# Two-layer hybrid decoder trunk: new costs in the order planner, and norm sums with one product

## The chip, the cores and the metric

The kernel runs on one core of a Trainium2 chip. The time is that of one launch on the device, in microseconds. Three runs of the kernel before took 1268.65, 1270.82 and 1272.52 us; the median, 1270.82 us, is the time to compare with.

In the profile PE is TensorE's matrix products and PEld its weight loads, DVE is VectorE, ACT ScalarE, POOL GpSimd and SP SyncE, which here issues most transfers (DMA).

## The reference

One sequence of 512 tokens, width 1024, with 16 learned tokens put ahead of it (528 columns), goes through two layers in float32. With `rms(x, g) = x / sqrt(mean(x^2) + 1e-6) * g` a layer is

```python
u = rms(h, pre_g);  z = u @ w_in                 # 1024 x 2824
y_attn = softmax(q k^T / 8 + F[t] - F[s], causal) v   # 8 heads of 64; F = cumsum(log_sigmoid(f + b))
y_conv = silu(layer_norm(conv31(a_val * sigmoid(a_gate)))) @ a_pw_w
y_sc   = sc_b * conv3(sc_c * sc_x)
y = head_norm(concat(y_attn, y_conv, y_sc)) @ w_out
h = h + rms(y, post_g)
z = conv3(rms(h, pre_g) @ w_up);  g, up = split(z)   # 2 x 2816 channels
h = h + rms((silu(g) * up) @ w_down, post_g)
```

All convolutions are causal and by channel. At the end the 16 learned tokens are dropped.

## The kernel before

**Layout.** Activations lie transposed: 128 partitions are 128 channels, the columns are the 528 tokens, worked on as two halves of 264 (`hf` 0 and 1). A float32 product of sufficient precision is made of three fast ones: each operand is split into a high part (a copy that rounds, on ScalarE) and a low part (a subtraction, on VectorE), and high x high, high x low and low x high are added up in PSUM (`mm3`, line 668). Weights come from memory block by block through a transfer on SyncE's queue, a copy on ScalarE (line 608) and a subtraction on VectorE (line 612). For 16 of the 22 channel blocks of the FFN's up projection, seven products of sums and differences stand in for eight (`ups`, line 2198).

**Stages.** An opening (norm of the input), then for either layer: the mixer (`mixer`: projections, attention, convolutions), the output projection with its two norms (`finish`), the FFN, and the FFN's last part with its norms (`finish` again).

**The norms.** `Norms.square` squares a pair of channel blocks (line 749) and adds it to an accumulator `acc` of 2 x 264 columns (line 765); after the last pair `acc` holds two partial sums side by side. `Norms.factor` sums over the channels with a matrix of 1/1024: one product for each of the two halves of `acc`, into the same PSUM columns (line 792). These two products have plain float32 operands. Some sums are taken in parts: with `apart`, the last pairs are not added to `acc` but get products of their own. Behind the sum stand three operations on ScalarE (lines 801 to 805) and two on VectorE (806, 812) that make the reciprocal root. The keys are `("h", hf)` for the norm ahead of a sub-layer and `("y", hf)` for the one behind it.

**The planner.** The order of the instructions on each engine isn't left to a compiler: `Flow` (lines 247 to 368) runs a small model of the chip while the kernel is built. Work for ScalarE, VectorE, GpSimd and SyncE is handed over with `flow.op(engine, us, fn, after, prio, lat)`: `us` is the time that it is thought to hold its engine, `lat` how much later than that its result is there, `after` what it waits for. `Flow.run` takes again and again what can start first, by priority where several can, and emits it; so its order becomes the engine's order. Products on TensorE come from Python generators that yield what they wait for; the first in the list of threads that can go on is emitted. Where the planner sees TensorE without work for longer than a limit, it emits filler products (line 1775), 80% of the gap at 0.225 us each. The chip then runs each engine's list in that order, and an instruction waits until its data are there.

The costs are simple formulas: `act_us(n)` is 0.17 + 0.0009 n, `dve_us(n)` 0.17 + 0.00101 n for n columns; a small transfer (`dma`, line 534) 0.35 us of SyncE. In the mixer a row maximum (`reduce` in `maxima`, line 1368) is booked with `dve_us(n) + 0.08`; the low parts of queries and keys (`low` in `q_proj` and `k_proj`, lines 1292 and 1320) with `dve_us(264)`; and the copy of a query's high part to other partitions with a landing of 2.2 us.

An engine is free for the next operation, in the model, where the one before ends:

```python
self.free[eng] = start + us
tok.time = start + us + lat
```

Of the kernel before, what the change touches and what calls it, by code (L numbers as in the profile page):

```python
# [9 lines left out]
F32 = mybir.dt.float32  # L10
# [10 lines left out]
H = L // 2  # L21
# [34 lines left out]
WE = 0.5  # L56
YS = (9, 9)
NWARM = 10
K1 = 2
SQD = (2, 6)  # L60
FILLED = 0.8
# [7 lines left out]
FILL_US = 0.225  # L69
OH = {(0, 0): -3, (0, 4): -2.9, (0, 6): -2.8, **{(1, k): -0.4 for k in range(0, KD, 2)}}  # L70
OW = (-0.46, -0.459)
ADD_US, ADD_LAT = 1.2, 3.6
PT = ((0.8035, 0.8055), (0.8035, 0.8055))
D0 = ((0, 0, 0, 0, 5, 10, 15, 20), (0, 0, 0, 0, 5, 10, 15, 20))

# [171 lines left out]
class Flow:  # L247
# [1 line left out]

    HOP = 0.06

    def __init__(self):
        self.pe = 0.0
# [52 lines left out]
    def run(self, stop=None):  # L308
        while True:
            if stop is not None and stop():  # L310
                return
            best = None
            for eng, ops in self.pend.items():
                can = [(r + self.HOP, o) for o in ops if (r := self.ready(o[4], o[7])) is not None]
                if can:
                    start = max(self.free[eng], min(r for r, _ in can))
                    o = min((o[0], r, o[1], o) for r, o in can if r <= start)[3]
                    if o[0] >= self.yields:
                        soon = [(r, q[0], q[1], q) for r, q in can if q[0] < o[0] - 0.5 and r < start + 0.6 * o[2]]
                        if soon:  # L320
                            start, _, _, o = min(soon)
                    if best is None or start < best[0]:
                        best = (start, eng, o)
            can = [(r, i) for i, t in enumerate(self.threads) if (r := self.ready(t[1])) is not None]
            if can:
                start = max(self.pe, min(r for r, _ in can))
                if best is None or start < best[0]:
                    best = (start, None, self.threads[min(i for r, i in can if r <= start)])
            if best is None:
                assert not self.threads and not any(self.pend.values()), "nothing can go on"  # L330
                return
            start, eng, o = best
            self.now = start
            if eng is not None:
                self.pend[eng].remove(o)
                _, _, us, fn, _, tok, lat, _, takes = o
                for r, slot in takes:
                    r.take(slot)
                fn()
                self.free[eng] = start + us  # L340
                tok.time = start + us + lat
                continue
            if self.rings and start > self.pe:
                bank = next((r.slots[0].buf for r in self.rings() if r.slots and r.slots[0].buf is not None
                             and (t := r.slots[0].time) is not None and t <= self.pe), None)
                if bank is not None:
                    gap = start - self.pe
                    for _ in range(int(FILLED * (gap - 0.05) / FILL_US) if gap > self.least else 0):
                        self.filler(bank)
            self.pe = max(self.pe, start)  # L350
            try:
                y = next(o[0])
            except StopIteration:
                self.threads.remove(o)
                continue
            o[1] = [Tok(0.0)] if y is None else [Tok(self.pe + y)] if isinstance(y, float) else y
# [30 lines left out]
def tile_hybrid_trunk(ctx: ExitStack, tc: tile.TileContext, xT, wflat, pv_d, out):  # L387
# [144 lines left out]
        return flow.op("pool", us, fn, after, **kw)  # L532

    def dma(out, in_, *after, **kw):
        return flow.op("sp", 0.35, lambda: nc.sync.dma_start(out, in_), after, **kw)

    class Early:

# [180 lines left out]
    class Norms:  # L719


        def __init__(self, pool, rs, nc=4, **apart):
            self.pool, self.nc = pool, nc
            self.c, self.acc = Ring(nc), Ring(2)
            self.factors(rs, **apart)

# [13 lines left out]
        def square(self, key, k, src, n, *after, prio=1, on_dve=False):  # L740

            apart = self.n_apart(key)
            s = self.sums.setdefault(key, {"parts": {}})
            us = act_us(2 * n)
            box, slot = {}, Slot()

            def squares(tile):
                box["c"] = tile()
                nc.scalar.activation(box["c"], src, AF.Square)

            if k == 0:
                a = act(us, lambda: squares(lambda: T(self.pool, [P, 2, H], F32, "acc", 2)[:, :, :n]), *after,
                        prio=prio, takes=[(self.acc, slot)])
                s["acc"], s["at"] = box, a
            else:
                if on_dve:
                    def product():
                        box["c"] = self.c_tile(n)
                        nc.vector.tensor_mul(box["c"], src, src)

                    a = dve(dve_us(2 * n), product, *after, prio=prio, takes=[(self.c, slot)])
                else:
                    a = act(us, lambda: squares(lambda: self.c_tile(n)), *after, prio=prio, takes=[(self.c, slot)])
                if k < KD - 2 * apart:
                    s["at"] = dve(dve_us(2 * n), lambda: nc.vector.tensor_add(s["acc"]["c"], s["acc"]["c"], box["c"]),
                                  a, s["at"], prio=prio)
                    slot.close(s["at"])
            if k == 0 or k >= KD - 2 * apart:
                s["parts"][max(0, k // 2 - KD // 2 + apart + 1) if k else 0] = box, slot
                box["at"] = [a]  # L770
            if k == KD - 2 * apart - 2:
                s["acc"]["at"], s["acc"]["there"] = [s["at"]], True
            return a

        def factor(self, key, n, out=None):
# [8 lines left out]
            for j in range(n_parts):  # L784
                yield [When(lambda: there(j)), When(lambda: self.after.get(key, []))]
                if j == 0:
                    p_slot = yield from flow.grab(pring[0]["n"])
                    ps = psum[:, p_slot.buf, :n]
                s = self.sums[key]
                box, slot = s["parts"][j]  # L790
                for i in range(2):
                    nc.tensor.matmul(ps, lhsT=om_d, rhs=box["c"][:, i, :], start=j + i == 0, stop=j + 1 == n_parts and i == 1)  # L792
                tok = flow.mm(2 * 0.0017 * n)
                slot.close(tok)
            s["free"] = mine = Slot()
            us, vs = act_us(n), dve_us(n)
# [97 lines left out]
    def mixer(l, ypool, first, close_first, spans):  # L894
# [384 lines left out]
        def q_proj(j):  # L1279
# [15 lines left out]
            def use(hf, ps, tok):  # L1295
                out = []
                for hd in (2 * j, 2 * j + 1):
                    c = half_sl(hf)
                    a = act(act_us(H), lambda hd=hd: high(hd, c, ps), tok, prio=0)
                    d = dve(dve_us(H), lambda hd=hd: low(hd, c, ps), a, prio=0)  # L1300
                    q_at.setdefault(hd, [zeros[hd]] if hd in zeros else []).append(a)
                    q2_at.setdefault(hd, []).append(d)
                    out += [a, d]
                return out

            yield from proj(use)
            for hd in (2 * j, 2 * j + 1):
                main = rows(hd)[0]
                q1, q2 = qh[hd % 4]
                q2_at[hd].append(dma(q2[main].bitcast(F32), q1[main].bitcast(F32), *q_at[hd], lat=2.2))  # L1310

        def k_proj(j):
            def high(hd, c, ps):
# [8 lines left out]
            def use(hf, ps, tok):  # L1322
                out = []
                for hd in (2 * j, 2 * j + 1):
                    c = half_sl(hf)
                    a = act(act_us(H), lambda hd=hd: high(hd, c, ps), tok, prio=0)
                    d = dve(dve_us(H), lambda hd=hd: low(hd, c, ps), a, prio=0)
                    q2_at[hd] += [a, d]
                    if hf == 0:
                        k_at[hd, 0] = a  # L1330
                    else:
                        k_at[hd] = [k_at[hd, 0], a]
                    out += [a, d]
# [11 lines left out]
        def maxima():  # L1345

            dm_at = {}
            for hd in range(HEADS):
# [6 lines left out]
                for b, (qs, n) in enumerate(QB):  # L1355
                    end = qs + n
                    pieces = [(0, end)] if end <= 512 else [(0, H), (H, end)]
                    for i, (a, z) in enumerate(pieces):
# [11 lines left out]
                                scalar=-3e38 if i == 0 else mcol[:n, 5:6], op0=ALU.add, op1=ALU.max,  # L1370
                                accum_out=mcol[:n, b:b + 1] if last else mcol[:n, 5:6])

                        d = dve(dve_us(z - a) + 0.08, reduce, tok, prio=0)
                        slot.close(d)
                        yield
                    diag.append(gp(0.5, lambda qs=qs, end=end, n=n, b=b: nc.gpsimd.tensor_scalar(
# [408 lines left out]
    with tc.tile_pool(name="pre", bufs=2, reuse_waits="tile") as sp, tc.manual_schedule(engines=every):  # L1785
# [7 lines left out]
        plan_w(after_mixer[0])  # L1793
        norms = Norms(sp, [T(sp, [P, L], F32, f"rs{i}", 1) for i in range(NRS)], NCS, h=APS)
        norms.apart["h", 0] = KD // 2 - 1
        hg, hg_at = T(sp, [P, KD, L], F32, "hg", 1), {}
        for hf in range(2):
            for k in range(0, KD, 2):
# [10 lines left out]
    for l in range(DEPTH):  # L1809
# [21 lines left out]
        with tc.tile_pool(name=f"fp{l}", bufs=2, reuse_waits="tile") as fp:  # L1831
# [29 lines left out]
            first = First(u_in, iws, {})  # L1861
            rs = T(fp, [P, L], F32, "rs", 1)
            norms = Norms(fp, [rs])
            plan = ExitStack()
            plan.enter_context(tc.manual_schedule(engines=every))
            flow.yields = YF[l]
# [551 lines left out]
            with plan:  # L2418
# [54 lines left out]
                wpos[0] += 2  # L2473
                rs, rz = (T(fp, [P, L], F32, n, 1) for n in ("rs", "rz"))
                norms.factors([rs, rz], h=APART)
                norms.apart["y", 1] = YA[l]
                norms.acc = Ring(2)
                flow.yields = YE[l]
# [60 lines left out]
```

## Time and profile before

| | |
|---|---|
| median of three runs | 1270.82 us (1268.65 to 1272.52) |
| profiled execution | 1272.24 us; span on the core 1270.5 us |
| busy PE | 1237.3 us, 97% of the span |
| busy PEld | 1187.7 us, 93% |
| busy DVE | 969.2 us, 76% |
| busy ACT | 775.3 us, 61% |
| busy POOL | 236.4 us, 19% |
| moved by DMA | 165.85 MB, 131 GB/s |
| mean granted clock of TensorE | 0.995 |

Busy time is the union of an engine's instructions in the profile. Matrix products overlap, and their ends are modelled, so a PE that is busy is not a PE at its peak. Lines such as L792 are lines of the kernel. In a group, `x64` counts instructions, behind the bar stand busy time, mean duration of one in ns, and the idle time of the engine just before them with what ended it. In a timeline a row starts with the time from the span's start and its length.

### The profile page before, as it was taken

To read this page: it belongs to the slowest core of one execution; us is meant where nothing else is said; L and a number is where in the kernel's file an instruction comes from. 1 tells how busy PE (TensorE), PEld (TensorE's weight loads), DVE (VectorE), ACT (ScalarE), POOL (GpSimd) and SP (SyncE) were. 2 spreads that over 40 slices of the span, in tenths; PEclk is the share of its full clock that TensorE was granted. 3 is DMA by queue.
4 is the path that set the end of the run, shared out by engine and by line. 5 is a ranking of instruction groups with operands and counts; after the bars stand their busy time and mean duration, and the time that the engine had idled before them with its cause. 6 is when DMAs were issued, how large, how long until landed. Compare 5 with 4: busy or idle time off the path is not lost.

```text
span 1270.5 us, 24515 instructions
## 1 busy us (share of the span) xinstructions
PE 1237.3 (97%) x9468; PEld 1187.7 (93%) x9468; DVE 969.2 (76%) x1752; ACT 775.3 (61%) x1571; POOL 236.4 (19%) x415
## 2 busy tenths in 40 slices
PE   8999999999999999999999999999998999999996
PEld 8999988999999999999999999889997999999996
DVE  7788877588866777778677888765897578778855
ACT  7257668667755555556673667685586565556552
POOL 1313321002122222120003233200022122112100
PEclk9999999999999999999999999999999999999998
DMA  6132231637486766776341322126376677668641
GB/s 226 51 102 60 63 89 34 218 113 169 106 194 139 191 160 147 170 162 184 114 141 35 95 80 68 56 74 206 128 171 144 155 163 170 165 146 180 142 142 67
DMA packets 73941, 165.85 MB, mean 131 GB/s; under 512 B 8080, under 2 KB 26640, under 8 KB 73312
## 3 DMA queue, kind: packets, MB, share of 16 engines
q1 hardware_dynamic: 52048, 124.86, 30.6%
q0 software_dynamic: 21360, 39.02, 18.9%
q8 instruction: 74, 1.21, 0.4%
q10 hardware_dynamic: 416, 0.40, 0.1%
q14 instruction: 43, 0.35, 0.1%
HBM read 129.14 MB, written 8.65 MB: 108 GB/s over the span
## 4 chain that ended last, share of the span: by engine, by line
PE 80%; DVE 6%; ACT 5%; DMA 5%; issue 3%; POOL 1%; SPq 0%; DVEq 0%; POOLq 0%; ACTq 0%
PE psum L668 37%; PE psum L2198 25%; PE psum L709 6%; PE psum L1204 4%; DMA raw<-in_w_dram 3%; PE psum L1462 2%; PE psum L1405 1%; PE psum L792 1%; DMA c<-acc 1%; PE psum L1361 1%; DVE wlo L612 1%; PE psum L1199 1%; DMA raw<-u 1%; POOL pf L1423 1%; ACT whi L608 1%
## 5 line engine op out<-in xcount | busy, mean ns | idle before, releaser
L668 PE MATMUL psum<-yhi,whi 128*128 128x264 f32 (+3 forms) x660 | 188.3, 300 | 3.1 <-ACT yp L2373 1.7
L668 PE MATMUL psum<-ylo,whi 128*128 128x264 f32 (+3 forms) x660 | 185.2, 295 | 1.1 <-DVE ylo L2175 0.8
L668 PE MATMUL psum<-yhi,wlo 128*128 128x264 f32 (+3 forms) x660 | 184.7, 295 | 0.1
L668 PE MATMUL psum<-uhi,whi 128*128 128x264 f32 (+1 forms) x640 | 165.1, 291 | 1.2 <-DVE q L1292 1.2
L668 PE MATMUL psum<-ulo,whi 128*128 128x264 f32 (+1 forms) x640 | 161.0, 284 | 0.1
L668 PE MATMUL psum<-uhi,wlo 128*128 128x264 f32 (+1 forms) x640 | 160.6, 283 | 0.0
L2124 DVE SCALAR_TENSOR_TENSOR c<-z,pv,c 128x528 f32<-128x528 f32 (+1 forms) x156 | 117.2, 758 | 29.3 <-ACT c L2122 26.5
L612 DVE TENSOR_TENSOR wlo<-raw,whi 128x1024 fp32r<-128x1024 f32 (+2 forms) x84 | 100.5, 1206 | 37.8 <-ACT whi L608 37.7
L668 PEld LDWEIGHTS psum<-yhi,whi 128*128 128x128 f32 x660 | 121.0, 189 | 8.4 <-ACT yp L2373 2.2
L668 PEld LDWEIGHTS psum<-ylo,whi 128*128 128x128 f32 x660 | 121.0, 189 | 4.4 <-DVE ylo L1088 1.1
L668 PEld LDWEIGHTS psum<-yhi,wlo 128*128 128x128 f32 x660 | 121.1, 189 | 3.2 <-DVE wlo L612 0.6
L668 PEld LDWEIGHTS psum<-uhi,whi 128*128 128x128 f32 x640 | 111.9, 188 | 4.3 <-issue 2.4
L668 PEld LDWEIGHTS psum<-ulo,whi 128*128 128x128 f32 x640 | 112.2, 188 | 0.5 <-DVE ulo L1947 0.3
L2211 ACT COPY z<-psum 128x264 f32<-128x264 f32 (+2 forms) x128 | 48.2, 377 | 105.4 <-PE psum L2198 104.7
L668 PEld LDWEIGHTS psum<-uhi,wlo 128*128 128x128 f32 x640 | 112.1, 188 | 0.0
L608 ACT CAST whi<-raw 128x1024 fp32r<-128x1024 f32 (+2 forms) x84 | 85.9, 1035 | 38.9 <-DMA raw<-in_w_dram 21.1
L937 DVE SCALAR_TENSOR_TENSOR cacc<-apad,pv,cacc 128x528 f32<-128x528 f32 x120 | 88.7, 768 | 0.3
L709 PE MATMUL psum<-uhi,whi 128*128 128x264 f32 (+1 forms) x320 | 85.0, 289 | 1.8 <-ACT uhi L840 1.8
L709 PE MATMUL psum<-uhi,wlo 128*128 128x264 f32 (+1 forms) x320 | 83.4, 283 | 0.0
L2052 DVE TENSOR_TENSOR wlo<-raw,whi 128x1024 fp32r<-128x1024 f32 (+4 forms) x78 | 76.6, 982 | 8.9 <-ACT whi L2049 8.3
L2049 ACT CAST whi<-raw 128x1024 fp32r<-128x1024 f32 (+4 forms) x78 | 66.4, 856 | 16.5 <-PE psum L668 10.3
L2198 PE MATMUL psum<-uhi,whi 128*128 128x264 f32 (+1 forms) x256 | 72.7, 284 | 2.2 <-ACT yp L2373 2.2
(317 smaller groups left out, 3729.2 us busy)
## 6 DMA issues: line engine op xcount, KB each, us to landing
raw<-in_w_dram SPq DMA_DIRECT2D x110, 512.0 KB
u<-in_w_dram SPq DMA_DIRECT2D x32, 512.0 KB
u<-in_w_dram POOLq DMA_DIRECT2D x32, 256.0 KB, 5.2
raw<-in_w_dram POOLq DMA_DIRECT2D x32, 256.0 KB, 4.0
u<-raw POOLq DMA_DIRECT2D x32, 256.0 KB, 3.8
raw<-u POOLq DMA_DIRECT2D x32, 256.0 KB, 4.4
raw<-in_w_dram SPq DMA_DIRECT2D x16, 448.0 KB
h_mid<-h SPq DMA_DIRECT2D x4, 1056.0 KB
```

Of the source, the lines that this page charges most:

```text
L608: nc.scalar.copy(box["hi"][:, :sz], box["raw"][:, :sz])
L612: nc.vector.tensor_sub(lo[:, :sz], box["raw"][:, :sz], box["hi"][:, :sz].bitcast(F32))
L668: nc.tensor.matmul(d, lhsT=w[a][:, k, cols], rhs=rhs(b, k, hf), start=start and i == 0 and p == 0, stop=stop and i == n - 1 and p == 2)
L709: nc.tensor.matmul(self.ps[hf, i], lhsT=self.ws[i].w[a][:, k, :], rhs=self.rhs(b, k, hf), start=k + a + b == 0, stop=k == KD - 1 and b == 1)
L937: nc.vector.scalar_tensor_tensor(conv[j], in0=src, in1=conv[j], scalar=col("a_dw_w", CK * j + i), op0=ALU.mult, op1=ALU.add)
L1204: nc.tensor.matmul(ps[:n, :nw], lhsT=(uhi, ulo)[ui][:, k, P * b:P * b + n], rhs=w[wi][:, k % 4, :], start=k == 0 and p == 0, stop=k == KD ...
L1462: nc.tensor.matmul(acc[:, s0 - qa:qz - qa], lhsT=vt[:, b].rearrange("p h d -> p (h d)")[:, o:o + P], rhs=pt, start=b == 0 and i == 0, stop ...
L2049: nc.scalar.copy(box[name][0], raw())
L2052: return a, dve(dve_us(n), lambda: nc.vector.tensor_sub(box[name][1], raw(), box[name][0].bitcast(F32)), a, prio=prio)
L2124: nc.vector.scalar_tensor_tensor(c, in0=z[:, i:i + n], scalar=wtap(i, t), in1=c, op0=ALU.mult, op1=ALU.add)
L2198: nc.tensor.matmul(d, lhsT=w[i][:, P * k:P * (k + 1)], rhs=terms[b][j][k](), start=start and k + p == 0, stop=k == KH - 1 and p == 2, skip ...
L2211: done[f, name] = act(us, lambda: nc.scalar.copy(z_of(f, e)[:, zin[h]], d[:, lo:]), *after, prio=0)
```

## The change

Costs in the planner: VectorE and ScalarE count as free 0.08 and 0.095 us before an operation of theirs ends (`OVER`), while the time at which the result is there stays. A small transfer holds SyncE for 0.55 us instead of 0.35 (`SP_US`), and the copy of a query's part lands 2.7 us later instead of 2.2 (`QLAT`). A row maximum holds VectorE 0.24 us beyond its formula, and its result is there 0.14 us before that (`RED`; before: 0.08 and 0). The low parts of queries and keys get 0.08 us more of the engine, with the result as early as before (`QK`).

Norm sums: for the keys in `folds`, the two halves of `acc` are added by VectorE once the last pair is in, and `factor` makes one product of it instead of two. The keys are `("h", 1)` in the opening, and `("y", 0)` and `("h", 0)` in each of the four `finish` stages, the last of which has no `("h", 0)`: eight sums.

`PFOLD` (0), `HOP_US` (0.06) and the two lines for `ADD_US` and `ADD_LAT` change no value.

```diff
+SP_US = 0.55
+QLAT = 2.7
+RED = (0.24, -0.14)
+QK = 0.08
+PFOLD = 0
+FOLD = ((("h", 1),), (("y", 0), ("h", 0)), (("y", 0), ("h", 0)))
+HOP_US = 0.06
+OVER = {"dve": 0.08, "act": 0.095}
...
-                self.free[eng] = start + us
+                self.free[eng] = start + us - OVER.get(eng, 0.0)
                 tok.time = start + us + lat
...
-        return flow.op("sp", 0.35, lambda: nc.sync.dma_start(out, in_), after, **kw)
+        return flow.op("sp", SP_US, lambda: nc.sync.dma_start(out, in_), after, **kw)
...
-            self.pool, self.nc = pool, nc
+            self.pool, self.nc, self.folds = pool, nc, ()
...
+            if k == KD - 2 * apart - 2 and key in self.folds:
+                def fold():
+                    t = s["acc"]["c"]
+                    nc.vector.tensor_add(t[:, 0, :], t[:, 0, :], t[:, 1, :])
+
+                s["at"] = dve(dve_us(n), fold, s["at"], prio=prio + PFOLD)
             if k == KD - 2 * apart - 2:
                 s["acc"]["at"], s["acc"]["there"] = [s["at"]], True
...
-                for i in range(2):
-                    nc.tensor.matmul(ps, lhsT=om_d, rhs=box["c"][:, i, :], start=j + i == 0, stop=j + 1 == n_parts and i == 1)
-                tok = flow.mm(2 * 0.0017 * n)
+                m = 1 if j == 0 and key in self.folds else 2
+                for i in range(m):
+                    nc.tensor.matmul(ps, lhsT=om_d, rhs=box["c"][:, i, :], start=j + i == 0, stop=j + 1 == n_parts and i + 1 == m)
+                tok = flow.mm(m * 0.0017 * n)
...
-                    d = dve(dve_us(H), lambda hd=hd: low(hd, c, ps), a, prio=0)
+                    d = dve(dve_us(H) + QK, lambda hd=hd: low(hd, c, ps), a, prio=0, lat=-QK)
...
-                q2_at[hd].append(dma(q2[main].bitcast(F32), q1[main].bitcast(F32), *q_at[hd], lat=2.2))
+                q2_at[hd].append(dma(q2[main].bitcast(F32), q1[main].bitcast(F32), *q_at[hd], lat=QLAT))
...
-                        d = dve(dve_us(z - a) + 0.08, reduce, tok, prio=0)
+                        d = dve(dve_us(z - a) + RED[0], reduce, tok, prio=0, lat=RED[1])
...
         norms.apart["h", 0] = KD // 2 - 1
+        norms.folds = FOLD[0]
...
             norms = Norms(fp, [rs])
+            norms.folds = FOLD[1]
...
                 norms.factors([rs, rz], h=APART)
+                norms.folds = FOLD[2]
                 norms.apart["y", 1] = YA[l]
```

(The line with `QK` changes twice, in `q_proj` and in `k_proj`.)

More of the change, by code (lines that the diff above doesn't have):

```diff
@@ L71 @@
 OW = (-0.46, -0.459)
-ADD_US, ADD_LAT = 1.2, 3.6
+ADD_US = 1.2
+ADD_LAT = 3.6
 PT = ((0.8035, 0.8055), (0.8035, 0.8055))
@@ L247 @@
 class Flow:
-    HOP = 0.06
+    HOP = HOP_US
     def __init__(self):
```

2 lines of the change are left out of this document (1 added, 1 removed).

## The prediction

> **What bounds the kernel now.** I read the page first, then the busy time cut into stages, then the list of who waited for whom on the matrix engine, and last the timeline at the longest stalls.
>
> ```profile
> span 1270.5 us, 24515 instructions
> PE 1237.3 (97%) x9468; PEld 1187.7 (93%) x9468; DVE 969.2 (76%) x1752; ACT 775.3 (61%) x1571; POOL 236.4 (19%) x415
> ```
>
> PE is busy for 1237.3 of 1270.5 us: 33.2 us idle in all. The stages (opening, mixer, output projection and FFN, of either layer, and the end) show where:
>
> ```profile
> 0.00:13.40 13.40, 10.85 (x58) 9.92 (x58) 6.99 (x17) 6.59 (x12) 3.58 (x23) 1.00 0.87 301
> ...
> 64.00:228.00 164.00, 160.72 (x1206) 149.30 (x1205) 132.82 (x326) 115.25 (x294) 41.08 (x89) 1.00 0.24 70
> 228.00:300.00 72.00, 71.65 (x573) 70.70 (x572) 53.83 (x85) 43.47 (x77) 3.40 (x4) 1.00 0.51 174
> 300.00:600.00 300.00, 297.60 (x2434) 296.36 (x2433) 232.57 (x356) 180.24 (x320) 60.11 (x71) 1.00 0.69 159
> 600.00:692.00 92.00, 90.38 (x698) 87.18 (x697) 66.24 (x105) 51.30 (x101) 12.19 (x35) 1.00 0.33 108
> 692.00:856.00 164.00, 160.56 (x1208) 149.21 (x1207) 132.70 (x326) 116.14 (x295) 40.65 (x85) 1.00 0.24 72
> ...
> 960.00:1216.00 256.00, 251.60 (x1751) 234.59 (x1750) 194.92 (x309) 146.11 (x271) 53.27 (x62) 1.00 0.70 157
> 1216.00:1257.80 41.80, 39.87 (x315) 39.24 (x313) 22.27 (x32) 18.61 (x32) 0.00 (x0) 0.96 0.31 111
> 1257.80:1270.50 12.70, 1.47 (x6) 0.68 (x4) 5.96 (x11) 2.84 (x6) 0.00 (x0) 0.66 0.25 83
> ```
>
> The columns are length, then busy time of PE, PEld, DVE, ACT and POOL with their instructions, the granted clock and DMA. The two ends (13.40 - 10.85 = 2.55, 12.70 - 1.47 = 11.23 us idle) are chains of latency around the first load and the last norm; no edit shortens an operation in them. What a better order can win lies between: 3.28 and 3.44 us of idle PE in the mixers (the rows of 164 us), 2.40 and 4.40 in the two FFN stages, 1.62 and 1.93 in the stages that follow them, 0.35 at 228. The waits name it:
>
> ```profile
> PE psum L668 <- ACT yp L2373: 2.6, 2, 1.7
> PE psum L2198 <- ACT yp L2373: 2.2, 2, 1.6
> PE psum L1385 <- POOL dm L1376: 1.9, 4, 0.7
> ...
> PE psum L668 <- DVE q L1292: 1.2, 2, 0.6
> ...
> PE psum L668 <- ACT yhi L2171: 1.1, 1, 1.1
> ...
> PE psum L792 <- DVE acc L765: 1.0, 3, 0.4
> ```
>
> Every one is short and comes a few times: the order on PE was written for a moment at which the other engine had not yet delivered. PE runs its list in order, so an item listed too early stops all behind it; one listed too late costs nothing by itself, except where the planner saw an empty PE and wrote filler products (line 1775) into it.
>
> One stall costs twice. Behind the idle time at 1220 to 1224 the clock falls:
>
> ```profile
> 1220.00:1222.00 2.00, 1.09 (x10) 0.89 (x8) 0.35 (x2) 1.31 (x2) 0.00 (x0) 1.00 1.07 376
> ...
> 1224.00:1226.00 2.00, 2.00 (x13) 2.00 (x12) 1.26 (x2) 1.22 (x2) 0.00 (x0) 0.58 0.78 276
> ```
>
> The stage's mean of 0.96 over 41.80 us is 0.04 x 41.80 = 1.7 us of work lost to it.
>
> **The change part by part.** *The eight folded sums.* Each takes one of the two ones-matrix products out of a norm sum (line 792) and puts one VectorE addition of 264 columns before it.
>
> ```profile
> 654.00 1.78 PE psum L792 x8
> ...
> L841 DVE TENSOR_TENSOR ulo<-yp,uhi 128x264 fp32r<-128x264 f32 x2 | 0.9, 430 | 0.2 <-ACT uhi L840 0.2
> ...
> 880.29 0.90 PE L792 MATMUL psum<-acc,om_d 128*128 128x250 f32 x3 [0.27 <-DVE acc L765]
> ```
>
> Eight PE instructions take 1.78 us, 0.2225 each; a product with float32 operands is two of them, so a fold frees 2 x 0.2225 = 0.445 us of PE, and eight free 3.56 us. The addition is 0.430 us on VectorE, in stages where that engine is busy for 53 to 75% (22.27 of 41.80, 53.83 of 72.00). It stands in the chain accumulation, fold, product, reciprocal root, so the sum is there 0.430 - 0.445, nearly the same, when the addition is taken at once. Seven of the sums are of the first half (only the opening's is of the second), and while they are made PE has the other half's products; that work covers the addition, and without it 0.430 us would come back for each. The wait of L792 for acc (1.0 us, three times) shows three sums listed before their accumulation was done; the one at 880, a first half's and so folded, may lose its 0.43 again. Between 0 gained (all eight in the open) and 3.56 I take 3.0: seven folds at their worth, less a little.
>
> *Overlap of 0.08 us (VectorE) and 0.095 us (ScalarE).* This moves no work, only the planner's clocks: an engine is taken as free that much before its operation ends. Whether that is so:
>
> ```profile
> 14.11 1.32 DVE L838 TENSOR_TENSOR hg<-hg,rs 128x528 f32<-128x528 f32 x2
> ...
> L838 DVE TENSOR_TENSOR hg<-hg,rs 128x528 f32<-128x528 f32 x7 | 4.7, 704 | 0.1
> ...
> 19.12 1.71 ACT L749 ACTIVATE c<-h 128x528 f32<-128x528 f32 x3
> ...
> L749 ACT ACTIVATE c<-h 128x528 f32<-128x528 f32 x19 | 11.8, 635 | 0.5 <-DMA h<-in_x_dram 0.5
> ```
>
> Two VectorE operations of 0.704 us lie in 1.32: 2 x 0.704 - 1.32 = 0.088 of overlap. Three ScalarE ones of 0.635 lie in 1.71: (1.905 - 1.71) / 2 = 0.098 each. The new numbers are the trace's. So the old plan believes both engines fuller than they are: in a mixer by 326 x 0.08 = 26 us of 164 on VectorE, whose busy time there is 132.8. The Trainium skill says otherwise (VectorE: DVE Perf Modes, section "The DRAIN you can't avoid"): behind each VectorE operation the pipe has to empty before the next one starts (it lets only some operations begin earlier). By that the new plan would be too hopeful by its whole correction and the result that of the third rival below; the trace does not agree, 0.088 us of overlap at line 838.
>
> What the old belief costs on PE is the mixers' idle time and the fillers:
>
> ```profile
> 9.35 2.62 PE L1775 MATMUL psum<-om_d 128*128 128x128 f32 x22
> ...
> L1775 PE MATMUL psum<-om_d x58: 270/275/317, 9.4 to 737.8; 128*128 128x128 f32 x58
> ```
>
> Of 58 fillers 22 lie in the opening, under a wait that stays (2.62 / 22 = 0.12 us each). The other 36, up to 737.7, are in the mixers, 18 each: 36 x 0.12 = 4.3 us. With the idle 3.28 + 3.44 that is 11.0 us in two mixers that a right plan could fill. A third is my choice, 3.7 us, because row maxima, matrix products and exponentials of one head wait for each other whatever the order. In the FFN stages and behind them 2.40 + 4.40 + 1.62 + 1.93 = 10.35 us are idle; most of it waits for the evacuations of yp, which themselves wait for transfers that the change does not touch, so a sixth, 1.7 us. Bounds: nothing at all (the list stays as good as it was), and 11.0 + 10.35 = 21 us; below nothing is the first rival.
>
> *Row maxima, query and key remainders, small transfers.* The reduction is booked with 0.24 - 0.08 = 0.16 us beyond its formula on the engine instead of 0.08.
>
> ```profile
> 84.69 0.43 DVE L1368 CUSTOM_DVE_ANT_0 junk<-psum,causal 128x272 bf16<-128x272 f32 x1
> ...
> 85.05 0.42 DVE L1010 TENSOR_TENSOR sccx<-psum,sccx 128x264 f32<-128x264 f32 x1
> 85.40 0.56 DVE L1368 CUSTOM_DVE_ANT_0 junk<-psum,causal 128x400 bf16<-128x400 f32 x1
> ...
> 86.11 0.43 DVE L1368 CUSTOM_DVE_ANT_0 junk<-psum,causal 128x264 bf16<-128x264 f32 x1
> ...
> L535 SPq DMA_DIRECT2D q<-q x16: 467/532/923, 71.8 to 786.9; - x16
> ```
>
> Behind another reduction it needs 86.11 - 85.40 = 0.71 us where the formula says 0.574 (0.17 + 0.00101 x 400), so 0.14 more: near the new entry. Before another operation it needs 85.05 - 84.69 = 0.36 where the formula says 0.445, so 0.08 less, and there the new entry is 0.24 us too careful. This delays nothing that runs; it only lists a few products later. A small transfer holds SyncE's queue 0.53 us (0.55 now, 0.35 before); it is as long as before on the chip, and what waits behind it in the queue (weight loads, other rows) gets a later place in the plan only. The landing is not shown; 2.2 or 2.7 us after the issue, no row of the waits names it, so between -0.5 and +0.5 us per layer I take 0.
>
> *Sum.* The profiled execution took 1272.24 us, 1.74 around its span. 1272.24 - 3.0 - 3.7 - 1.7 = 1263.8. It lies 1.4 above the median of the runs (1270.82), so I say 1263 where 1262.4 follows, leaning to the careful side of two choices of mine.
>
> **The rivals.** *First, slower: the plan turns hopeful where ScalarE does not overlap.* Evacuations that write part of the partitions show no overlap:
>
> ```profile
> 88.75 0.87 ACT L1387 CAST q<-psum 1x264 fp32r<-1x264 f32 x2
> 89.64 0.78 ACT L1287 ACTIVATE q<-psum 64x264 fp32r<-64x264 f32 x2
> ...
> L1287 ACT ACTIVATE q<-psum 64x264 fp32r<-64x264 f32 x32 | 12.3, 385 | 4.6 <-PE psum L668 4.1
> L1315 ACT CAST k<-psum 64x264 fp32r<-64x264 f32 x32 | 11.9, 373 | 9.7 <-PE psum L668 9.0
> L1387 ACT CAST q<-psum 1x264 fp32r<-1x264 f32 x32 | 11.3, 370 | 7.6 <-PE psum L1385 5.5 <-PE psum L1405 1.3
> ```
>
> Two of 0.385 take 0.78, two of 0.370 take 0.87. The change corrects VectorE's remainders for this (0.08 added back) but not these 96 of ScalarE; each is now believed over 0.095 us early, and the PSUM bank that it empties with it. If all 96 are met by a product already listed, PE stands 9.1 us more: 1272.24 - 3.0 + 9.1 = 1278.3, against the median 1277. It becomes slower than a measurement can tell from 72 of them on ((3.8 + 3.0) / 0.095). For it: queries wait already (L668 for q, 1.2 us). Against: ScalarE stands idle 4.6 to 9.7 us before these groups, and an idle engine's early release moves nothing.
>
> *Second: the order stays as good as it is, only the folds count.* The sum without the last two terms is 1272.24 - 3.0 = 1269.2, against the median 1268. For it: 97% busy leaves little.
>
> *Third: VectorE does not overlap after all.* Then 64 remainders and sums that free PE's banks come 0.083 us later than listed, 5.3 us: 1272.24 - 3.0 + 5.3 = 1274.5, against the median 1273. The rows speak against it.
>
> *Fourth: the stall at 1220 to 1224 goes too.* Its idle time, 1.93 us in the stage, and the 1.7 us of the slow clock: 1263.8 - 1.9 - 1.7 = 1260, and with more than a third in the mixers 1256. For it: one long chain of ScalarE and VectorE by turns ends there. Against: nothing in the change is aimed at it.
>
> **How the numbers follow.** A change below 0.3%, 3.8 us, cannot be told from none here. The forecast has 0.56, its own range 1258 to 1267; the first rival 0.17, the second 0.18, the third 0.02, the fourth 0.07. Faster is the forecast and the fourth, 0.63; same the second and third, 0.20; slower the first, 0.17. The range runs from 1254, a little under the fourth, to 1276, just inside the first.
>
> **What would show it.** Line 792 with 84 instructions instead of 100, and eight more VectorE additions of 264 columns; fewer than 36 fillers in the mixers, and mixers of 160 to 162 us in place of 164; the wait of PE for q and dm shorter. The forecast is wrong if the mixers stay at 164 (second rival), if PE waits longer for ScalarE's q and k (first), or if the waits of L792 for acc grow by 0.43 a sum (the folds in the open).

## The result and the profile after

The changed kernel took 1278.6 us (median of four runs, 1276.43 to 1279.13), the kernel before 1270.4 us in the runs beside it: the ratio is 1.0061, with an interval of 1.0042 to 1.0079. It is slower, by some 8 us, where 1263 was forecast. Its profiled execution took 1278.29 us. The head of its page:

```profile
span 1276.6 us, 24449 instructions
PE 1235.4 (97%) x9432; PEld 1183.6 (93%) x9432; DVE 969.5 (76%) x1760; ACT 772.0 (60%) x1571; POOL 234.1 (18%) x415
```

PE is busy for 1.9 us less than before (1237.3 - 1235.4) and idle for 8.0 us more (1276.6 - 1235.4 = 41.2, against 33.2). 8.0 - 1.9 is the 6.1 us that the span grew. PE has 36 instructions fewer (9468 - 9432): 16 of the folds and 20 fillers. So no work was added; PE waits. The same stretches of time as before, in the same columns:

```profile
64.00:228.00 164.00, 157.38 (x1159) 144.79 (x1158) 128.87 (x321) 109.12 (x285) 39.49 (x87) 0.99 0.23 68
228.00:300.00 72.00, 70.46 (x561) 69.22 (x561) 50.50 (x83) 43.49 (x81) 1.88 (x4) 1.00 0.49 168
300.00:600.00 300.00, 296.53 (x2415) 294.24 (x2414) 230.84 (x356) 179.33 (x318) 61.93 (x72) 1.00 0.67 153
600.00:692.00 92.00, 89.02 (x692) 86.47 (x692) 67.09 (x102) 55.24 (x105) 8.61 (x23) 1.00 0.41 136
692.00:856.00 164.00, 157.24 (x1173) 145.68 (x1172) 130.88 (x323) 107.48 (x279) 43.08 (x98) 1.00 0.22 68
856.00:960.00 104.00, 102.36 (x834) 100.42 (x833) 81.37 (x134) 70.19 (x124) 9.09 (x11) 1.00 0.56 162
960.00:1216.00 256.00, 254.26 (x1777) 237.77 (x1777) 195.58 (x308) 149.06 (x276) 54.62 (x64) 1.00 0.70 159
1216.00:1257.80 41.80, 39.75 (x329) 39.28 (x329) 26.07 (x39) 21.82 (x37) 0.00 (x0) 1.00 0.34 114
```

In the mixers' windows the idle time doubled: 164 - 157.38 = 6.62 us (3.28 before) and 6.76 (3.44), and 47 and 35 fewer products went through in the same time (1206 - 1159, 1208 - 1173). Of the other rows shown, only the second FFN won: 1.74 us idle where there were 4.40. The stretches are fixed, and the changed kernel runs later in them (by 9.8 us at the end of the second mixer), so this split is rough. The waits of PE in the changed kernel (in total, times, longest):

```profile
PE psum L1478 <- ACT sq L1495: 5.1, 4, 2.2
PE psum L1377 <- DVE mcol L1384: 4.5, 6, 0.9
PE psum L1401 <- POOL dm L1392: 2.3, 2, 1.1
```

The rows nearest to the first two in the list of before:

```profile
PE psum L1462 <- ACT yta L1480: 1.7, 4, 0.6
...
PE psum L1361 <- DVE mcol L1368: 0.2, 1, 0.2
```

The first names the other evacuation of the same bank, the second the same wait. So these two kinds of wait, 1.9 us before, are 9.6 us now. Both are in the attention: line 1478 weighs the values with the exponentials and waits until ScalarE has emptied the bank of the part before (line 1495); line 1377 makes the products whose row maxima VectorE takes (line 1384) and waits for a free bank. The list has no row for a query or key on ScalarE, the wait on which the first rival rested (the one row for a query before names VectorE, line 1292). The longest stall of PE, first as ScalarE's timeline shows it:

```profile
199.00 1.03 ACT L1589 CAST yhi<-cacc 128x264 fp32r<-128x264 f32 x3
199.94 1.04 ACT L617 CAST whi<-raw 128x1024 fp32r<-128x1024 f32 x1
201.00 0.28 ACT L1495 ACTIVATE sq<-psum 128x128 f32<-128x128 f32 x1
```

and of PE:

```profile
201.34 1.70 PE L1478 MATMUL psum<-pf,vals 128*128 128x400 f32 x2 [2.17 <-ACT sq L1495]
...
836.45 0.94 PE L1478 MATMUL psum<-pf,vals 128*128 128x400 f32 x2 [2.17 <-ACT sq L1495]
```

The bank waits on ScalarE behind three roundings of the convolution's end and a weight copy of 1.04 us. PE stands for 2.17 us, in either mixer, since what follows in its list is of the same chain.

Where the time goes by stage is seen best from two points in each mixer: the first product of row maxima and the last products of a head norm. Before:

```profile
82.50 0.34 PE L1361 MATMUL psum<-k,q 128*16 128x16 f32 x2
...
219.27 0.67 PE L1532 MATMUL psum<-sq,hsel 128*64 128x264 f32 x4
...
709.70 0.34 PE L1361 MATMUL psum<-k,q 128*16 128x16 f32 x2
...
846.61 0.67 PE L1532 MATMUL psum<-sq,hsel 128*64 128x264 f32 x4
```

After:

```profile
81.90 0.34 PE L1377 MATMUL psum<-k,q 128*16 128x16 f32 x2
...
222.37 0.67 PE L1548 MATMUL psum<-sq,hsel 128*64 128x264 f32 x4
...
716.97 0.34 PE L1377 MATMUL psum<-k,q 128*16 128x16 f32 x2
...
856.42 0.67 PE L1548 MATMUL psum<-sq,hsel 128*64 128x264 f32 x4
```

The mixers last 140.47 and 139.45 us between these rows (222.37 - 81.90, 856.42 - 716.97), 136.77 and 136.91 before: 6.2 us more, against 6.1 in the span. What the other stages lose (4.2 us between the mixers) and win (3.7 us behind the second, 0.6 ahead of the first) comes to nothing.

### The profile page after: what moved, and what is told of

Same layout as the page of the kernel before. It is cut to its first block, busy times and chain, and to the rows that moved or that the text cites. A ratio compares the mean times of both kernels' runs of the same rounds, so it can differ in the third digit from the quotient of the medians.

```text
span 1276.6 us, 24449 instructions
## 1 busy us (share of the span) xinstructions
PE 1235.4 (97%) x9432; PEld 1183.6 (93%) x9432; DVE 969.5 (76%) x1760; ACT 772.0 (60%) x1571; POOL 234.1 (18%) x415
## 4 chain that ended last, share of the span: by engine, by line
PE 68%; DVE 10%; ACT 7%; issue 7%; DMA 5%; POOL 1%; SPq 0%; DVEq 0%; POOLq 0%; ACTq 0%
PE psum L677 31%; PE psum L2216 21%; PE psum L718 5%; PE psum L1220 4%; PE psum L1478 2%; DMA raw<-in_w_dram 2%; DVE cacc L953 2%; ACT whi L617 1%; DMA c<-acc 1%; PE psum L1421 1%; DMA raw<-u 1%; DVE wlo L2070 1%; POOL dm L1392 1%; DVE ulo L1965 1%; PE psum L1377 1%
## 5 line engine op out<-in xcount | busy, mean ns | idle before, releaser
L617 ACT CAST whi<-raw 128x1024 fp32r<-128x1024 f32 (+2 forms) x84 | 85.7, 1034 | 41.2 <-DMA raw<-in_w_dram 18.0
```

The source lines that it names most:

```text
L617: nc.scalar.copy(box["hi"][:, :sz], box["raw"][:, :sz])
```

## The experiments

Two theories stood against each other, named by letters in the expectations. A: the size or meaning of the new costs decides, so that each has a price of its own. C: the planner takes the first thing that can start, so any change of a cost gives another order from there on, and the time is a draw from orders of different quality, whatever the new number means. For the last three runs D and E were added: D, a few entries in front of which PE stands are the loss; E, a wait that is taken away is waited again at the next dependency. Where an expectation has another letter, it says what it stands for.

### The parts alone

```diff
# folds only: old costs
+SP_US = 0.35; QLAT = 2.2; RED = (0.08, 0.0); QK = 0.0; OVER = {}
# overlap only: the other old costs, no folds
+FOLD = ((), (), ())
# costs only: RED, QK, SP_US, QLAT new, no folds
+FOLD = ((), (), ()); OVER = {}
# no folds: all new costs
+FOLD = ((), (), ())
```

> The eight folded sums with all planner costs as before. If a fold is worth its product (0.445 us of PE), 1270.4 - 3 = 1267.4 us, between 1266.8 and 1270.4. If the additions lie in the open or the folds reorder a stage badly, 1272 to 1278 and the folds carry part of the loss of 8.2 us.

> Only the overlap of 0.08 and 0.095 us, other costs and sums as before. Theory A (the overlap makes the plan too hopeful): 1274 to 1280 us, both mixers 2 to 4 us longer, PE waiting for row maxima and for the evacuations of the weighted sums. Theory B (the new cost of row maxima and small transfers does it): 1265 to 1271, mixers no longer than before. Theory C (any change of cost reshuffles the order and the parts do not add up): anything, but the three parts alone do not add up to +8.2 within 3 us.

> Only the new costs of row maxima, of query and key remainders and of small transfers; no overlap, no folds. Theory A: 1269 to 1272 us, mixers as before. Theory B: 1274 to 1280 and mixers 2 to 4 us longer. Theory C: as for the overlap alone.

> The changed kernel without the folded sums. If the folds bring what they are worth, 1278.6 + 3 = 1281.6 us; if they cost time in the changed order, 1274 to 1278.

Measured: folds only 1270.69 us (ratio 1.0009, 0.9999 to 1.0018); overlap only 1276.22 (1.0052, 1.0032 to 1.0072); costs only 1288.29 (1.0148, 1.0133 to 1.0163); all but the folds 1280.0 (1.008, 1.0065 to 1.0095). The overlap alone costs 0.5%, the other costs alone 1.5%, both together 0.8%. That the parts do not add up is what theory C says. It doesn't decide alone: `RED` and `QK` each hold 0.08 us that is there to take the overlap back, so without `OVER` these costs are too careful by their design, and part of the 1.5% can have that cause. The folds alone neither harm nor help by more than a measurement tells; within all the new costs, leaving them out gave 1.4 us more, where their worth was put at 3.

### A nudge, and two costs one by one

The hop is the planner's time for a signal between engines; it exists in the planner alone.

```diff
# old costs, no folds, and one cost changed in each:
+HOP_US = 0.061                        # 0.06
+OVER = {"dve": 0.001, "act": 0.001}   # {}
+SP_US = 0.55; QLAT = 2.7              # 0.35, 2.2
+RED = (0.24, -0.14)                   # (0.08, 0.0)
```

> [...] Theory A (the size of the new costs decides): 1268 to 1271 us, as before. Theory C (any change reshuffles the order, and the order before was a lucky one): it moves by 3 us or more, most likely up, 1272 to 1290, with the mixers' ends displaced.

> All costs and sums as before, but an overlap of 0.001 us for both engines instead of none, an 80th of the change's. Theory A: 1268 to 1271 us. Theory C: 3 us or more away from before, and as far as the full overlap alone (1276.2) or farther.

> Only the costs of small transfers (0.55 us of the queue, landing 2.7). Of the 18 us that the new costs alone lose, theory A says that one of them carries it by its meaning: here 1269 to 1272 if it is the row maxima, 1284 to 1290 if it is the transfers. Theory C: some value between 1270 and 1290 that does not add up with that of the row maxima alone.

> Only the cost of row maxima (0.24, result 0.14 earlier). Theory A: 1284 to 1290 us if this carries the loss of the new costs, 1269 to 1272 if the transfers do. Theory C: between 1270 and 1290, and not adding up to 1288 with the transfers alone.

Measured: 1272.29 us (1.0018, 1.0006 to 1.0029), 1284.4 (1.0108, 1.009 to 1.0126), 1283.02 (1.0098, 1.0081 to 1.0114) and 1287.41 (1.0131, 1.0114 to 1.0148). The hop of 0.061 came out between the theories, 2.7 us above the 1269.6 beside it. An overlap of a single nanosecond, an 80th of the measured one, costs 1.1%, twice what the overlap at its measured size costs. Small transfers and row maxima cost 1.0 and 1.3% alone; in the run that has both and the remainders 1.5%. Theory A falls with that. In the order made by one nanosecond the longest wait is the one seen after the change:

```profile
PE psum L1478 <- ACT sq L1495: 6.0, 2, 3.0
```

### The changed kernel, nudged

```diff
+HOP_US = 0.059                                          # first
+HOP_US = 0.066                                          # second
+HOP_US = 0.0606; OVER = {"dve": 0.088, "act": 0.092}; ADD_US = 1.060   # third
```

The third is the order whose end the planner itself puts earliest, among some 200 that differ in such small numbers.

> The changed kernel with the planner's hop at 0.059 instead of 0.060 us. Theory A (the new costs as such lose): 1277 to 1280 us, as the changed kernel. Theory C (the loss is one order out of many): 3 us or more away from 1278.6; by the planner's own end of its plan, which is shorter here, 1271 to 1275.

> The changed kernel with the hop at 0.066 us, whose plan the planner itself believes longer than the changed kernel's. Theory A: 1277 to 1280 us. Theory C: 1282 to 1290.

> The changed kernel with an overlap of 0.088 and 0.092, a hop of 0.0606 and 1.060 us for an accumulating transfer's issue: of some 200 such small variations the one whose plan the planner believes shortest. Theory A: 1276 to 1280 us. Theory C: 1266 to 1272, so no slower than before: picking an order brings back what the change lost.

Measured: 1271.28 us (0.9998, 0.9986 to 1.001), 1285.61 (1.011, 1.0095 to 1.0125) and 1272.41 (1.001, 0.9999 to 1.002). With the new costs too, one nanosecond in the hop moves the time by 7 us, six nanoseconds by as much the other way. Theory C holds: the new costs can give an order as good as before, and the one that they gave is not it. Picking by the planner's own end gave a good order (0.4 us above the range expected), but none better than before. That end pointed the right way each time (see the expectations), shorter for the first nudge and longer for the second; between the good orders it did not decide, since its shortest plan took 1272.41 us and another 1271.28.

### The folds with the order kept

The fold is issued together with the last accumulation, and the planner books two products as before; so all else stands as in the kernel before.

```diff
+                    def add():
+                        t = s["acc"]["c"]
+                        nc.vector.tensor_add(t, t, box["c"])
+                        if k == KD - 2 * apart - 2 and key in self.folds:
+                            nc.vector.tensor_add(t[:, 0, :], t[:, 0, :], t[:, 1, :])
...
+                tok = flow.mm(2 * 0.0017 * n)
```

> The eight folded sums put into the order of before: the addition of 264 columns is emitted behind the last accumulation, the planner is told nothing of it and books two products as before, so every other instruction stays where it was. This is what the folds themselves do. The prediction's term: 1270.4 - 3.0 = 1267.4 us. Rival (the additions lie in the open, what PE gains it waits for): 1269 to 1271. Rival (the additions are late where PE waits): 1271 to 1273.

Measured: 1270.14 us against 1271.07 (0.9991, 0.9981 to 1.0001), so 0.9 us, not clear of none, where the eight sums were to free 3.56 on PE. The products stand in PE's list in the order of before, without the sixteen that are gone. Each fold does free what it was to free; one of them, before and with the fold:

```profile
272.03 1.05 PE L792 MATMUL psum<-acc,om_d 128*128 128x264 f32 x4
...
271.35 0.61 PE L807 MATMUL psum<-acc,om_d 128*128 128x264 f32 x2
```

Behind each of the eight the next products come 0.42 to 0.45 us earlier, 3.5 us in all. The waits of PE for its norm sums show that the additions were hardly in the way:

```profile
PE psum L807 <- ACT c L758: 1.2, 2, 0.6
...
PE psum L807 <- DVE acc L776: 0.9, 2, 0.4
```

They are what they were (1.2 and 1.0); beside them two of the eight products wait for their addition, 0.7 us together. But the time is given back further on. In the stage from 228 us PE is idle for 72 - 71.20 = 0.80 us instead of 0.35, and a wait stands in the list that was not there before:

```profile
228.00:300.00 72.00, 71.20 (x568) 70.09 (x568) 54.61 (x87) 43.34 (x76) 3.42 (x4) 1.00 0.52 173
...
PE psum L718 <- ACT uhi L893: 0.7, 2, 0.4
```

PE comes earlier to a product in its list, and that one waits for another engine (here ScalarE's rounding of the next sub-layer's input, behind the norm), whose own chain has not become shorter. This accounts for part of what did not come through. The rest can't be told apart: in the FFNs, where no fold lies, the two profiled executions drift against each other by up to 1.1 us at a single product.

### Only the entries that PE waits for, moved

Here the order of the changed kernel is kept, and a few entries are issued later than planned, right behind the operation that they stood in front of. Lines of `Flow.run`:

```diff
-                fn()
+                k = self.count[eng] = self.count.get(eng, -1) + 1
+                if (eng, k) in LATE:
+                    self.held.append((LATE[eng, k], fn))
+                else:
+                    fn()
+                for w, f in [h for h in self.held if h[0] == (eng, k)]:
+                    f()
+                self.held = [h for h in self.held if h[0] != (eng, k)]
```

> The changed kernel with its costs and its order; by hand, in either mixer, only a few entries of ScalarE's list change places: the weight copy (line 617) ahead of one evacuation of the weigh product, and the weight copy and three roundings of the convolution's end (line 1589) ahead of another, are issued right behind that evacuation (line 1495) instead of ahead of it. Theory D (a few such inversions are what the changed order loses): the wait of PE for sq falls from 5.1 us to under 1, the half clock at 201 goes: 2 x (2.17 + 0.39 - 0.3) + 1.7 = 6.2 us less than the changed kernel, 1272.4. Theory E (what a wait gives back is waited at the next dependency, as with the eight folds, where 0.9 of 3.0 us came through): a third or less of it, 1276.5 or more.

> As the run before it, and in either mixer the row maxima (line 1384) at three places are issued ahead of what stood in front of them on VectorE (a convolution tap, a query's remainder, two taps with two key remainders), and two clearings of query rows on GpSimd behind the two diagonals of row maxima. Theory D: the waits of PE for mcol (4.5 us) and dm (2.3 us) fall by two thirds, 4.5 us less than the run before it, 1268 and so below the kernel before. Theory E: at most 1.5 us less than the run before it.

> The changed kernel planned with a hop of 0.059 us (1271.28 us, as before), and in either mixer two places changed by hand in the same way: a copy out of PSUM (line 1496), for which PE waited 0.87 us, ahead of two operations that stood waiting for GpSimd in front of it, and the first row maxima ahead of an addition of 264 columns. Theory D: 2 x (0.87 + 0.35) = 2.4 us less than with that hop alone, 1268.9, a little below the kernel before. Theory E: under 0.8 us less.

Measured: evacuations first 1279.73 us (1.0067, 1.0052 to 1.0082); with the row maxima too 1279.31 (1.0067, 1.0053 to 1.0081); the order of hop 0.059 with its two waits moved 1270.69 (0.9991, 0.998 to 1.0002), 0.6 us below that hop alone, which was measured beside other runs; no version was found that is faster than before by more than its interval. Theory D falls: with the evacuations first PE is idle for 40.8 us in all (1278.1 - 1237.3), against 41.2 in the changed kernel, as theory E has it. Part of that kernel's time may be clock: its profiled execution spent 6.8 us at half clock in either mixer, the changed kernel 3.4 in one. But its two executions with the highest mean clock, 0.994, still took 1278.92 and 1276.87 us, not 1272.4. In the first of these kernels (lines here are 9 higher than in the changed one) the waits for sq are gone from the head of the list, and another stands there:

```profile
PE psum L1487 <- POOL pf L1448: 4.7, 2, 2.4
PE psum L1386 <- DVE mcol L1393: 4.4, 6, 0.9
```

PE's timeline at the same place:

```profile
199.59 0.65 PE L1430 MATMUL psum<-q,k 128*128 128x144 f32 x2
202.61 1.27 PE L1487 MATMUL psum<-pf,vals 128*128 128x272 f32 x2 [2.38 <-POOL pf L1448]
```

and GpSimd's:

```profile
201.32 1.95 POOL L1448 TENSOR_SCALAR_AFFINE_SELECT pf<-pf 128x128 f32<-128x128 f32 x2 [11.53 <-ACT pf L1441]
```

The bank is emptied early; now the convolution's roundings and two weight copies stand in front of the exponentials instead, the causal mask on GpSimd comes as much later, and PE waits 2.38 us for it in place of 2.17 for the bank. In the second kernel the waits for mcol leave the head of the list in the same way, and one for the low part of the exponentials takes their place:

```profile
PE psum L1487 <- POOL pf L1448: 4.8, 2, 2.4
PE psum L1487 <- DVE pl L1464: 3.9, 2, 1.9
```

In these two kernels a stall of this kind is a place where PE's list holds only products of one serial chain (logits, exponential, mask, product, evacuation), and what is taken from one link is waited for at the next.

### All runs beside each other

The mixers' length is taken from the trace of each kernel: from the first product of row maxima to the start of the last product of a head norm (attention's or convolution's, whichever is later), both mixers together, against before.

| kernel | mixers, us | span, us | ratio of times |
|---|---|---|---|
| hop 0.059, moved | -1.4 | -3.5 | 0.9991 |
| folds, old order | +0.1 | -1.9 | 0.9991 |
| hop 0.059 | -1.0 | -1.7 | 0.9998 |
| folds only | +0.1 | -1.7 | 1.0009 |
| picked order | -0.8 | -0.2 | 1.0010 |
| old costs, hop 0.061 | +1.8 | -1.2 | 1.0018 |
| overlap only | +5.3 | +4.8 | 1.0052 |
| the changed kernel | +6.3 | +6.1 | 1.0061 |
| evacuations first | +9.2 | +7.6 | 1.0067 |
| evacuations and maxima first | +5.8 | +6.5 | 1.0067 |
| no folds | +6.1 | +5.9 | 1.0080 |
| small transfers only | +8.5 | +9.5 | 1.0098 |
| old costs, overlap 0.001 | +16.1 | +13.0 | 1.0108 |
| hop 0.066 | +10.8 | +13.7 | 1.0110 |
| row maxima only | +17.3 | +15.2 | 1.0131 |
| costs only | +8.6 | +16.6 | 1.0148 |

With one exception (costs only) the span follows the mixers within 3.1 us. So it is the order inside the mixers that decides here; the stages around them change too, but nearly cancel. The clock does not tell the orders apart: hop 0.066 has a mean granted clock of 0.996 in its profile, the kernel before 0.995, and its span is 13.7 us longer. In seven of the slow orders the last heads' attention comes late. Products of line 1478 (1462 before) in the last part of the first mixer, before:

```profile
204.00:232.00 28.00, 2.96 (x10) 1.61 (x10) 1.00 0.27 86
```

after:

```profile
204.00:232.00 28.00, 5.66 (x20) 2.76 (x18) 0.99 0.16 50
```

and in the order of hop 0.059:

```profile
204.00:232.00 28.00, 0.00 (x0) 0.00 (x0) 1.00 0.36 117
```

After the change 20 of them come there instead of 10, when the other products are nearly used up and the chain has nothing to lie beside. The second mixer, counted from 121.5 us behind its first product of row maxima, has 18 where before has 10 and hop 0.059 has 3. It isn't the only way to lose: with the overlap alone 5 are left in the first mixer, and it is the convolutions' head norms that end late (last product at 221.67 us, 215.22 before); hop 0.066 and the costs only have 10 in either mixer, as before, counted so.

## Why the prediction was wrong

**The mixers, -3.7 us: the sign was wrong, +6.2.** This is the step that failed. The prediction read the planner as if better costs gave a better order, and bounded the gain by the idle time and the fillers that a right plan could fill, with a loss only through the first rival. But the planner doesn't search; it takes what can start first. The order before was one good order of the old costs: all five kernels with those costs slightly or partly changed, the overlap at its measured size apart, are slower, four of them by about 1% or more. The changed costs gave an ordinary order of theirs. "Nothing at all" was no lower bound; one nanosecond of overlap, by the runs, costs 14 us.

**"One listed too late costs nothing by itself".** This sentence failed with it. Late entries go with the loss: in the second mixer the last product of row maxima starts 822.1 - 716.97 = 105.1 us behind the first, before 809.3 - 709.70 = 99.6, and the last heads' chain ends the mixer with little beside it. The groups of line 1361 before

```profile
L1361 PE MATMUL psum<-k,q x96: 170/287/475, 82.5 to 809.3; 128*128 128x264 f32 x32, 128*16 128x16 f32 x16, 128*128 128x144 f32 x16, 128*128 128x272 f32 x16
```

and of line 1377 after (duration in ns, first and last start):

```profile
L1377 PE MATMUL psum<-k,q x96: 170/288/482, 81.9 to 822.1; 128*128 128x264 f32 x32, 128*16 128x16 f32 x16, 128*128 128x144 f32 x16, 128*128 128x272 f32 x16
```

A late entry costs here once what is listed before it runs out. Fewer fillers were no sign of a better mixer either: line 1791 has 38 instructions instead of 58, 22 in the opening as before and 8 in each mixer, fewer than 36 as forecast, while PE's idle time doubled. In the groups of PE's instructions after:

```profile
L1791 PE MATMUL psum<-om_d 128*128 128x128 f32 x38 | 4.8, 277 | 0.0
```

**The folds, -3.0 us: the price of one was right, what comes through was wrong, 0.9 and not clear of none.** The instructions went as predicted, 48 + 36 = 84 in line 808:

```profile
L808 PE MATMUL psum<-acc,om_d 128*128 128x264 f32 (+2 forms) x48 | 14.0, 401 | 0.0
L808 PE MATMUL psum<-c,om_d 128*128 128x264 f32 (+1 forms) x36 | 9.0, 391 | 1.5 <-ACT c L758 1.5
```

Their additions are hidden, as predicted (with the order kept, all but 0.7 us in two of them): the wait for acc didn't grow by 0.43 a sum. But the term took PE's freed time for the kernel's, though the stages around have idle PE of their own; with the order kept, a part of the freed time is seen to turn into waits further on.

**The FFN stages and those behind them, -1.7 us: nothing came.** Their idle PE was 2.40 + 1.62 + 4.40 + 1.93 = 10.35 us; it is 3.47 + 2.98 + 1.74 + 2.05 = 10.24, lost in the first layer and won in the second.

**Row maxima, remainders, transfers, 0.** The reading of the costs stands (0.71 us behind another reduction), the price does not: the transfers alone cost 1.0%, the row maxima alone 1.3%, in the mixers above all (8.5 of 9.5 us; 17.3, of which 2.1 came back elsewhere).

**The first rival** had the sign and nearly the time (1277), but not the place, so its time is luck: no wait for ScalarE's queries and keys stands in the list, and as large a loss comes where no overlap is booked at all. Nor does the edit by itself free a bank earlier, as this rival has it: the time at which a result is there stays, and only what is queued behind it is planned earlier. The wait that spoke for it (1.2 us) was for VectorE. **The second** gave the folds 3 us, of which 0.9 came with the order kept. **The third** is not borne out: with the overlap booked, hop 0.059 is as fast as before. (Its 0.083 us stands in no row; the rows give 0.088, the change books 0.08.) **The fourth:** the slow clock at 1220 to 1224 did go (0.96 to 1.00 in that stage), but its idle time did not (1.93 to 2.05), and a slow stretch came in the mixer, below.

Open stays whether the new costs are better over many orders: the five with all of them (as they are, without folds, and nudged three times, one of these picked) lie between 1271.28 and 1285.61, the old ones' neighbours between 1272.29 and 1288.29, too few to tell. Which of its decisions makes the planner put the last heads late was not found.

## What to carry to other kernels

Where a greedy planner writes the order, a change of a cost is not an edit with a mechanism but a new draw; predict it with both signs, wide, and with odds against it when the order before is better than its neighbours, as here. Compare the planner's own end of both plans first: in the three nudges it gave the sign. Nudge a number by a nanosecond before believing any explanation of such a result, and measure an edit's own worth with the order held fixed. A stall names the link of a chain that happened to be last; before mending that link, look whether the next one is any earlier.

## What was not expected of the hardware

The clock can fall to half after a short stall, in the middle of dense work. In the changed kernel it follows the 2.17 us at line 1478:

```profile
200.00:202.00 2.00, 0.66 (x1) 0.50 (x2) 1.74 (x4) 1.98 (x4) 0.00 (x0) 0.82 0.00 0
202.00:204.00 2.00, 2.00 (x6) 1.18 (x5) 1.99 (x3) 0.61 (x2) 0.00 (x0) 0.50 0.38 104
204.00:206.00 2.00, 1.80 (x11) 1.20 (x9) 0.93 (x3) 0.71 (x3) 0.77 (x3) 0.82 0.90 277
```

(2 x 0.18 + 2 x 0.50 + 2 x 0.18) / 0.5 = 3.4 us at half clock, so at most 1.7 us of work, nearly as much as the stall. The stall of 2.17 us at 836.45 in the second mixer brought none, so length alone does not decide. In the run with the costs only it lasted longer:

```profile
228.00:232.00 4.00, 2.91 (x12) 2.66 (x12) 2.79 (x8) 2.72 (x8) 0.00 (x0) 0.66 1.03 329
232.00:236.00 4.00, 2.92 (x14) 2.66 (x13) 2.08 (x6) 2.41 (x6) 0.26 (x4) 0.50 0.42 148
236.00:240.00 4.00, 4.00 (x22) 4.00 (x22) 1.63 (x2) 3.82 (x6) 0.00 (x0) 0.56 0.00 0
```

That is (4 x 0.34 + 4 x 0.50 + 4 x 0.44) / 0.5 = 10.2 us at half clock, and a second stretch of 6.8 us follows near 868 us. Yet they don't explain what the mixers' length leaves out in that run (16.6 - 8.6 = 8.0): the profiled execution, with a mean clock of 0.991, took 1288.92 us, and three others of the same kernel, with 0.995, took 1287.98 to 1288.52. PE waits in a part of these stretches anyway (it is busy for 2.91 and 2.92 us of 4). In the kernel before it is otherwise: of its 29 executions beside the kernel with the order kept, the six with a mean clock of 0.997 took 1269.1 us on average, the four with 0.994 took 1274.2. So a slow stretch is to be priced by other executions of the same kernel, not by its length alone. The Trainium skill (TensorE: Matmul & The Clock Gate, section "Part 1: The HAM clock gate (the "warmup" mystery)") has the clock fall after an idle window of about 3.4 us. The length of the slow stretch, 3.4 us or three times that, fits such a window; the stall ahead of it was shorter here, 2.17 us.
